# A one-core trunk layer: own buffers for value rows, stores of G behind the weights, x1 loaded early

## The chip, the core and the metric

The kernel runs on one core of one Trainium2 chip. The metric is the device time of one execution in microseconds. Three runs of the kernel before took 1787.8, 1790.84 and 1793.23 us, median 1790.84.

## The reference, cut to what matters

One layer on 512 tokens of width 2048. Four kinds of token mixing are computed first and projected back; then comes a gated feed-forward network with a convolution over three tokens. The change touches the second half:

```python
x = x + rms_norm(mixed, norm_gains[l, 1])          # this x is "x1"
h = rms_norm(x, norm_gains[l, 2])
x = x + rms_norm(conv_geglu_ffn(h, ffn_w_up[l], ffn_conv_w[l], ffn_w_down[l]), norm_gains[l, 3])

def conv_geglu_ffn(h, w_up, conv_w, w_down):
    u = causal_dwconv(h @ w_up, conv_w)            # 2 x 4096 columns
    g, up = jnp.split(u, 2, axis=-1)
    return (jax.nn.gelu(g, approximate=True) * up) @ w_down
```

The product `gelu(g) * up` is called G here: 32 rows of 128 features, each a tile of 128 partitions by 512 tokens (256 KB). Everything is in float32.

## The kernel before, in words

Features lie on partitions and tokens along the free dimension. Each weight and each operand is split into two parts, hi and lo (a cast on ScalarE, L99, L177 or L1008, and a subtraction on VectorE, L100, L178 or L1009), and each product is made of hi times hi, hi times lo and lo times hi. A plain stage (`group`, L125 to L170) loads a weight chunk of 512 KB (L98), splits it and lets TensorE run 24 or more matmuls per chunk into four PSUM tiles.

The order on TensorE is the order in which the program is written. Other engines' instructions are put in order by a scheduler with a model of times; those under `tc.high_priority` (weight loads, splits, evictions) go ahead of the rest where they are ready. `tc.issue_after(i)` puts instructions behind `i` on the same engine. Each engine, SP with its DMA issues included, takes its instructions strictly in the order so fixed: what waits holds up all behind it. A tile from a pool of n buffers has to wait until the last use of the tile that had its place is over, a store's landing included. `at` and `tick` (L107 to L114) hang side work on TensorE's progress.

The stages that matter, with their time in the profile:

- Up projection, plain (to 857 us): the first four gate rows and four value rows of G. `up_plain` (L964) runs four times: each half of the tokens H0, H1 (256 each), and in each first the gate columns (half 0), then the value columns (half 1). Evictions go to `ub` tiles (L969). When a row's second token half is there, `done` calls `conv` (L943): y = first tap (ScalarE, L948), two more taps (VectorE, L950), and for the gate the gelu (ScalarE, L953). `glu` (L957) multiplies the value by its gate (VectorE, L958) and stores the row to `g_d` in DRAM on the SP queue (L959). Gate and value rows y all come from `t2()`, the pool t2f of six buffers.
- Up projection, units 4 to 31 (857 to 1424 us): `up_unit` (L1096) makes one row of G by `seven` (L1023), a Strassen scheme of seven products on half-size blocks in the order 11, 21, T2, T1, T3, 22, T4. A product is eight pairs: eight matmuls of 512 columns (L1039) and eight of 256 (L1044). Products go to three PSUM tiles x, y, w; `take` (L1099) evicts each (ScalarE copy L1103 for a first term, VectorE adds L1105 and L1106). Weights: five plain loads by SP (L1002) and three accumulating DMAs by GpSimd (L1018) per unit. TensorE yields before T4, and there `conv` of the gate is written; `conv` of the value and `glu` follow T4. From here on `t2()` is the pool t2s and `up_tile` the pool ubs, four buffers each, made where the norms' pool `norm_ph` has just been closed (L987 to L989).
- Down projection (1424 to 1768 us): first four plain groups over G's rows 0 to 3, then `seven` again for rows 4 to 19 (`down_unit`, L1195, with operands T1, T2, T3 in the places a2, a1, a3 and spare weights in a0), then four last groups over rows 20 to 31 (`last_group`, L1219), the fourth once for each token half. `load_g` (L1135) brings G's rows back through `ystage`.
- Last norm and output: the squares of each output row (L798, ScalarE) are summed by GpSimd (L802), except the last ones, which enter TensorE's sum over partitions directly (`SumSq`, L789; the third number of its call says how many). `finish` (L1230) takes rstd (L188 to L194) and then for four blocks q loads x1 from DRAM (L1236) into one of three tiles (`x1p`, two of `ystage`), scales (L1240), adds (L1241) and stores the output (L1242), two rows at a time. `finish` runs once per token half.

Of the kernel before, what the change touches and what calls it, by code (L numbers as in the profile page):

```python
# [9 lines left out]
F32 = mybir.dt.float32  # L10
F32R = mybir.dt.float32r
AF = mybir.ActivationFunctionType
ALU = mybir.AluOpType
# [3 lines left out]
P = 128  # L17
S = 512
D = 2048
KT = D // P  # L20
# [4 lines left out]
HALVES = (slice(0, S // 2), slice(S // 2, S))  # L25
# [23 lines left out]
def trunk(ctx: ExitStack, tc: tile.TileContext, xT, params, consts, wgate, w_in, w_out, w_up0, w_up, w_dn, w_dns, out):  # L49
    nc = tc.nc  # L50
    V, A, G, T = nc.vector, nc.scalar, nc.gpsimd, nc.tensor
# [3 lines left out]
    act = ctx.enter_context(tc.tile_pool(name="act", bufs=1))  # L55
# [21 lines left out]
    def pc(name, i=0):  # L77
        return par[:, PC[name] + i:PC[name] + i + 1]
# [7 lines left out]
    w_split, w_load = [], []  # L86
# [17 lines left out]
    beside = {}  # L104
# [67 lines left out]
    def repeated(t, n):  # L172
        return t.unsqueeze(1).broadcast_to([P, n, t.shape[-1]])
# [27 lines left out]
    def traced():  # L201
        return len(nc.cur_bb.bb.instructions)

    def after_act(mark):
        held_back[:] = [i for i in list(nc.cur_bb.bb.instructions)[mark:] if type(i).__name__ == "InstActivation"]
# [13 lines left out]
    x1_d = [dram.tile([P, 2, 4, S // 2], F32, name=f"x1_d{q}") for q in range(4)]  # L219
    g_d = [dram.tile([P, S], F32, name=f"g_d{k}") for k in range(FF // P)]  # L220
# [4 lines left out]
    with ExitStack() as ph:  # L225
        big = ph.enter_context(tc.tile_pool(name="big", bufs=19))
        t2p = ph.enter_context(tc.tile_pool(name="t2p", bufs=8))
# [4 lines left out]
        def t2(dt=F32):  # L232
            return t2p.tile([P, S], dt, name="t2")
# [137 lines left out]
        for i in range(2):  # L371
            V.tensor_tensor(out=lmp[:, i * 64:(i + 1) * 64], in0=par[:, dl + 128 * i:dl + 128 * i + 64],
                            in1=par[:, dl + 128 * i + 64:dl + 128 * i + 128], op=ALU.mult)
# [9 lines left out]
        def lru(pair, xs, gs):  # L383
# [41 lines left out]
            def scan():  # L425
# [9 lines left out]
                after_act(mark)  # L435

            at(t0 + 1, conv)
            at(t0 + 9, lambda: gates(blocks[0]))
            at(t0 + 13, lambda: gates(blocks[1]))
# [181 lines left out]
        ys, vs = {}, []  # L621
# [150 lines left out]
    with ExitStack() as ph:  # L772
        wide = ph.enter_context(tc.tile_pool(name="wide", bufs=2))
        ystage = ph.enter_context(tc.tile_pool(name="ystage", bufs=2))
        up_ph = ph.enter_context(ExitStack())
        neg_p = up_ph.enter_context(tc.tile_pool(name="neg_p", bufs=1))
        t2p = up_ph.enter_context(tc.tile_pool(name="t2f", bufs=6))
        ubp = up_ph.enter_context(tc.tile_pool(name="ubp", bufs=8))

        norm_ph = up_ph.enter_context(ExitStack())  # L780
# [99 lines left out]
        H0, H1 = HALVES  # L880
# [25 lines left out]
        def split_t2():  # L906

            with tc.high_priority(offset=AHEAD):
                for i in range(2):
                    split(mg[2 + i][1], actq[i][:, 0, :, H1], actq[i][:, 1, :, H1])  # L910
# [22 lines left out]
        def up_tile():  # L933
            t = ubp.tile([P, 514], F32, name="ub")
            V.memset(t[:, 0:2], 0.0)  # L935
            return t
# [6 lines left out]
        def conv(t, half, unit, minus=False):  # L943
            def tap(i):
                n = 3 * unit + i
                return neg_w[:, n:n + 1] if minus else pc("ffn_w", 96 * half + n)
            y = t2()
            A.activation(out=y, in_=t[:, 0:512], func=AF.Copy, scale=tap(0))  # L948
            for i in (1, 2):
                V.scalar_tensor_tensor(out=y, in0=t[:, i:i + 512], scalar=tap(i), in1=y, op0=ALU.mult, op1=ALU.add)  # L950
            if half == 0:
                mark = traced()
                A.activation(out=y, in_=y, func=AF.Gelu_apprx_tanh)  # L953
                after_act(mark)
            return y

        def glu(unit, gate, value):  # L957
            V.tensor_tensor(out=value, in0=value, in1=gate, op=ALU.mult)  # L958
            nc.sync.dma_start(out=g_d[unit], in_=value)  # L959


        ub, gates = {}, {}
# [1 line left out]
        def up_plain(half, ts):  # L964
            def evac(u, ps):
                if ts.start == 0:
                    ub[half, u] = up_tile()
                t = ub[half, u]
                A.copy(out=t[:, 2 + ts.start:2 + ts.stop], in_=ps)  # L969
                return (lambda: done(u)) if ts.stop == S else None  # L970

            def done(u):
                y = conv(ub[half, u], half, u)
                if half == 0:
                    gates[u] = y
                else:
                    glu(u, gates[u], y)
            group([w_up0[half, c] for c in range(8)], act_h, act_l, natural, evac,
                  mm_tile if half == 0 else pa_tile, ts)

        for ts in HALVES:
            for half in range(2):
                up_plain(half, ts)


        split_t2()
        norm_ph.close()  # L987
        t2p = up_ph.enter_context(tc.tile_pool(name="t2s", bufs=4))
        ubp = up_ph.enter_context(tc.tile_pool(name="ubs", bufs=4))  # L989
        spare_t = wide.tile([P, 4, 4, S // 2], F32, name="mg")  # L990
        spare = [spare_t[:, i] for i in range(4)]
        turn = [0]
# [103 lines left out]
        def up_unit(unit):  # L1096
            u = [up_tile(), up_tile()]

            def take(i, ts, ps, first):  # L1099
                t = u[i][:, 2 + ts.start:2 + ts.stop]  # L1100
                with tc.high_priority(offset=AHEAD):
                    if first:
                        A.copy(out=t, in_=ps[:, 0:256])  # L1103
                    else:
                        V.tensor_tensor(out=t, in0=t, in1=ps[:, 0:256], op=ALU.add)  # L1105
                    V.tensor_tensor(out=t, in0=t, in1=ps[:, 256:512], op=ALU.add)  # L1106

            steps = seven(w_up[unit - 4], tops, take, first=unit == 4)
            next(steps)
            gate = conv(u[0], 0, unit)  # L1110
            for _ in steps:
                pass
            glu(unit, gate, conv(u[1], 1, unit, minus=True))

        for unit in range(4, FF // P):
            up_unit(unit)
        up_ph.close()


# [4 lines left out]
        m3 = [m3p.tile([P, 4, S], F32, name=f"m3{q}") for q in range(4)]  # L1124
# [10 lines left out]
        def load_g(k, t):  # L1135

            for i in range(0, 4, 2):
                with tc.high_priority(offset=AHEAD):
                    split(load_pair(k + i), t[:, 0, i:i + 2], t[:, 1, i:i + 2])
                for n in range(i, i + 2):  # L1140
                    g_h[k + n], g_l[k + n] = t[:, 0, n], t[:, 1, n]
# [66 lines left out]
            down_unit(n)  # L1208
        build_ph.close()

        x1p = ph.enter_context(tc.tile_pool(name="x1p", bufs=1))
        ph2 = ph.enter_context(tc.tile_pool(name="ph3", bufs=1))
        rstd3 = ph2.tile([P, S], F32, name="rstd3")
        load_g(20, wide.tile([P, 2, 4, S], F32R, name="xs"))
        load_g(24, wide.tile([P, 2, 4, S], F32R, name="xs"))
        load_g(28, act.tile([P, 2, 4, S], F32R, name="a1"))
        ss3 = [SumSq("q3", 4, 2), SumSq("q3", 4, 2)]

        def last_group(g, hfs, ts, pool_tile):  # L1219
            def evac(u, ps):  # L1220
                m = m3[g][:, u, ts]
                V.tensor_tensor(out=m, in0=m, in1=ps, op=ALU.add)
                done = [ss3[hf].add(m3[g][:, u, HALVES[hf]]) for hf in hfs]
                A.activation(out=m, in_=m, func=AF.Copy, scale=gain(3, 4 * g + u))
                for hf, d in zip(hfs, done):
                    if d:
                        at(clock[0] + 4, lambda hf=hf: finish(hf))
            group([w_dn[g, c] for c in range(2, 8)], g_h, g_l, range(20, 32), evac, pool_tile, ts)

        def finish(hf):  # L1230
            ts = HALVES[hf]
            ss3[hf].rstd(rstd3[:, ts])
            for q in range(4):
                x1 = (x1p if q == 0 else ystage).tile([P, 2, S], F32, name="ys")
                x1 = x1.rearrange("p a (b t) -> p (a b) t", b=2)
                nc.sync.dma_start(out=x1, in_=x1_d[q][:, hf])  # L1236
                for i in range(2):
                    ks = slice(2 * i, 2 * i + 2)
                    t, x = m3[q][:, ks, ts], x1[:, ks]
                    V.tensor_tensor(out=t, in0=t, in1=repeated(rstd3[:, ts], 2), op=ALU.mult)  # L1240
                    V.tensor_tensor(out=x, in0=t, in1=x, op=ALU.add)  # L1241
                    (nc.scalar if i else nc.sync).dma_start(out=out[hf, 2 * q + i], in_=x)  # L1242

        for g in range(3):
            last_group(g, (0, 1), ALL, mm_tile if g % 2 == 0 else pa_tile)
# [117 lines left out]
```

## Time and profile before

The profiled execution took 1794.26 us; its span, from the first to the last recorded event, is 1792.5 us.

| | |
|---|---|
| median of three runs | 1790.84 us |
| profiled execution, span | 1794.26, 1792.5 us |
| granted TensorE clock, mean | 0.986 |
| TensorE busy | 1734.0 us (97%) |
| VectorE, ScalarE, GpSimd busy | 1245.2, 896.1, 160.6 us |
| DMA | 308.13 MB, mean 172 GB/s |

The profile page gives busy times, a row of 40 slices, and the chain of waits that ended last. The trace behind it can be asked for waits by engine, for a timeline of instructions (start, duration, engine, line, operation, output<-input, and in brackets the idle time before and what ended it), and for busy times in chosen windows. PE is TensorE, PEld its weight loads, DVE VectorE, ACT ScalarE, POOL GpSimd, SPq the DMA queue of SyncE. Names are the program's: `f` is the tile of `t2()` in the feed-forward part, `ub` the tile before the convolution, `m` an output row, `ys` a staging tile, `x_d` x1 in DRAM.

### The profile page before, as it was taken

How to read it: one execution, taken by the hardware profiler on the slowest of the kernel's cores; microseconds unless marked ns; L12 is line 12 of the kernel's file. 1: busy time of each engine (PE TensorE's matmuls, PEld its weight loads, DVE VectorE, ACT ScalarE, POOL GpSimd, SP SyncE). 2: the span in 40 equal slices, each digit the busy share in tenths (PEclk: the TensorE clock that was granted, in tenths of full speed). 3: DMA queues.
4: the chain of work that ended last, by engine and by line, in shares of the span. 5: the costliest groups of instructions: out<-in, count | busy, mean ns of one | idle time of the engine just before them, and what ended most of it. 6: DMA issues, size and time to landing. Idle time of an engine off the chain costs nothing.

```text
span 1792.5 us, 25050 instructions
## 1 busy us (share of the span) xinstructions
PE 1734.0 (97%) x9504; PEld 1504.4 (84%) x9504; DVE 1245.2 (69%) x1903; ACT 896.1 (50%) x1335; POOL 160.6 (9%) x228
## 2 busy tenths in 40 slices
PE   8999999999999999999699999999999999999994
PEld 7778788887888889999588888888888878888884
DVE  7884576666666324889788888788888886775336
ACT  6442676655334334777355555555555563333432
POOL 0000011100000111100011111111111001110210
PEclk9999999999999999999899999999999999999997
DMA  7224222242222635775688888988888668876245
GB/s 259 83 94 142 82 77 77 88 144 92 95 85 92 200 105 179 235 233 178 190 212 241 229 227 228 232 228 216 232 238 224 199 196 232 217 200 196 94 129 177
DMA packets 97025, 308.13 MB, mean 172 GB/s; under 512 B 10469, under 2 KB 14821, under 8 KB 96905
## 3 DMA queue, kind: packets, MB, share of 16 engines
q1 hardware_dynamic: 80056, 247.29, 41.1%
q0 software_dynamic: 15696, 57.15, 17.3%
q10 hardware_dynamic: 1152, 2.10, 0.3%
q8 instruction: 74, 1.21, 0.3%
q14 instruction: 47, 0.38, 0.1%
HBM read 265.59 MB, written 21.24 MB: 160 GB/s over the span
## 4 chain that ended last, share of the span: by engine, by line
PE 86%; DMA 5%; DVE 3%; issue 3%; ACT 3%; SPq 0%; POOL 0%; DVEq 0%; ACTq 0%; POOLq 0%
PE mm L150 32%; PE mm L1039 25%; PE mm L1044 13%; PE pa L150 5%; PE mm L121 2%; PE mm L123 2%; PE mm L122 2%; PE pa L575 1%; DMA xs<-mg 1%; DMA a<-in_w_dns_dram 1%; DMA ys<-x_d 1%; DMA g_d<-f 1%; DVE w_lo L100 1%; DVE vd L267 1%; ACT w_hi L99 1%
## 5 line engine op out<-in xcount | busy, mean ns | idle before, releaser
L100 DVE TENSOR_TENSOR w_lo<-w_raw,w_hi 128x1024 fp32r<-128x1024 f32 (+1 forms) x207 | 253.3, 1225 | 260.9 <-PE mm L150 142.7
L150 PE MATMUL mm<-a,w_hi 128*128 128x512 f32 (+1 forms) x1744 | 373.0, 364 | 2.8 <-DVE t L318 2.1
L99 ACT CAST w_hi<-w_raw 128x1024 fp32r<-128x1024 f32 (+1 forms) x207 | 215.7, 1045 | 296.2 <-PE mm L150 216.0
L150 PEld LDWEIGHTS mm<-a,w_hi 128*128 128x128 f32 x1744 | 297.7, 189 | 53.8 <-DVE t L318 2.6
L1039 PE MATMUL mm<-a,w_hi 128*128 128x512 f32 x1088 | 276.2, 396 | 20.7 <-DVE ub L935 13.5
L1008 ACT CAST w_hi<-w_raw 128x1024 fp32r<-128x1024 f32 x145 | 152.2, 1050 | 205.7 <-PE mm L1039 168.1
L1039 PEld LDWEIGHTS mm<-a,w_hi 128*128 128x128 f32 x1088 | 197.7, 191 | 57.0 <-DVE ub L935 13.7
L1009 DVE TENSOR_TENSOR w_lo<-w_raw,w_hi 128x1024 fp32r<-128x1024 f32 x145 | 177.0, 1221 | 39.2 <-ACT w_hi L1008 38.8
L150 PE MATMUL mm<-a,w_lo 128*128 128x512 f32 (+1 forms) x872 | 198.9, 367 | 0.0
L150 PEld LDWEIGHTS mm<-a,w_lo 128*128 128x128 f32 x872 | 147.7, 190 | 24.3 <-issue 1.5
L1044 PEld LDWEIGHTS mm<-a,w_lo 128*128 128x128 f32 x1088 | 150.1, 192 | 10.8
L1044 PE MATMUL mm<-a,w_lo 128*128 128x256 f32 x1088 | 153.3, 284 | 0.0
L1039 PE MATMUL mm<-xs,w_hi 128*128 128x512 f32 x576 | 144.3, 392 | 0.2 <-DVE ub L1106 0.2
L1008 ACT CAST w_hi<-mg 128x1024 fp32r<-128x1024 f32 x84 | 87.7, 1044 | 86.8 <-PE mm L1039 84.2
L1039 PEld LDWEIGHTS mm<-xs,w_hi 128*128 128x128 f32 x576 | 103.7, 189 | 19.0 <-DVE ub L1106 0.4
L1009 DVE TENSOR_TENSOR w_lo<-mg,w_hi 128x1024 fp32r<-128x1024 f32 x84 | 102.5, 1220 | 24.3 <-ACT w_hi L1008 24.3
L1039 PE MATMUL mm<-mg,w_hi 128*128 128x512 f32 x352 | 88.9, 395 | 1.2 <-DVE m L1201 1.2
L1044 PEld LDWEIGHTS mm<-xs,w_lo 128*128 128x128 f32 x576 | 78.6, 190 | 5.6
L1106 DVE TENSOR_TENSOR ub<-ub,mm 128x256 f32<-128x256 f32 x196 | 81.2, 414 | 1.5 <-ACT ub L1103 1.5
L1044 PE MATMUL mm<-xs,w_lo 128*128 128x256 f32 x576 | 80.3, 282 | 0.0
L1039 PEld LDWEIGHTS mm<-mg,w_hi 128*128 128x128 f32 x352 | 64.0, 191 | 12.8 <-ACT a L177 1.4
L150 PE MATMUL pa<-a,w_hi 128*128 128x256 f32 (+1 forms) x512 | 72.3, 294 | 0.7 <-ACT w_hi L99 0.7
(267 smaller groups left out, 2554.8 us busy)
## 6 DMA issues: line engine op xcount, KB each, us to landing
w_raw<-in_w_up_dram SPq DMA_DIRECT2D x115, 512.0 KB, 5.1
w_raw<-in_w_in_dram SPq DMA_DIRECT2D x87, 512.0 KB, 3.5
mg<-in_w_up_dram SPq DMA_DIRECT2D x56, 512.0 KB, 4.2
w_raw<-in_w_out_dram SPq DMA_DIRECT2D x48, 512.0 KB, 3.5
w_raw<-in_w_dn_dram SPq DMA_DIRECT2D x38, 512.0 KB, 3.5
w_raw<-mg POOLq DMA_DIRECT2D x28, 512.0 KB, 5.6
mg<-in_w_up_dram POOLq DMA_DIRECT2D x27, 512.0 KB, 7.9
w_raw<-in_w_up_dram POOLq DMA_DIRECT2D x27, 512.0 KB, 9.0
```

Of the source, the lines that this page charges most:

```text
L99: w_split.append(A.copy(out=hi[:, sl], in_=raw[:, sl]))
L100: V.tensor_tensor(out=lo[:, sl], in0=raw[:, sl], in1=hi[:, sl].bitcast(F32), op=ALU.subtract)
L121: T.matmul(ps, lhsT=sh, rhs=mh, start=first, stop=False)
L122: T.matmul(ps, lhsT=sh, rhs=ml, start=False, stop=False)
L123: T.matmul(ps, lhsT=sl, rhs=mh, start=False, stop=last)
L150: T.matmul(pss[u], lhsT=a, rhs=b, start=c == 0 and kk == 0 and not low and i == 0, stop=False)
L267: V.tensor_tensor(out=ssum, in0=ssum, in1=sq, op=ALU.add)
L1008: w_split.append(A.copy(out=by4(hi), in_=v))
L1009: V.tensor_tensor(out=by4(lo), in0=v, in1=by4(hi).bitcast(F32), op=ALU.subtract)
L1039: T.matmul(ps.rearrange("p (a t) -> p a t", a=2), lhsT=hi[:, k * P:(k + 1) * P], rhs=tops[name][k], start=first and k == 0, stop=False, **kw)
L1044: T.matmul(ps[:, 0:256], lhsT=lo[:, k * P:(k + 1) * P], rhs=tops[name][k][:, 0], start=False, stop=k == 7, **kw)
L1106: V.tensor_tensor(out=t, in0=t, in1=ps[:, 256:512], op=ALU.add)
```

## The change

Four things:

1. Value rows in `conv` come from a pool of their own, `t2s` with four buffers named v2; gates stay in `t2()`, the six buffers of t2f, to the end of the up projection. For that the norms' pool is closed, and t2s and ubs are made, between the two token halves of the plain stage instead of after it.
2. `glu` no longer stores a row at once; it puts the store on a list. `store_g` issues what is on the list, behind the last weight load written so far. It is called in `up_unit` after the gate's `conv` of the next unit, and once after the last unit.
3. x1 is loaded whole, by eight DMAs of 512 KB, into two tiles in the places a0 and a2 as soon as the Strassen units of the down projection leave them, and behind the last weight load written by then. `finish` reads and writes x1 there; `x1p` is gone.
4. The last sums of squares: the last three rows of each token half, instead of the last two, go directly to TensorE's sum and not through GpSimd's running sum (five buffers instead of four).

```diff
-            y = t2()
+            y = t2() if half == 0 else t2s.tile([P, S], F32, name="v2")
...
         def glu(unit, gate, value):
             V.tensor_tensor(out=value, in0=value, in1=gate, op=ALU.mult)
-            nc.sync.dma_start(out=g_d[unit], in_=value)
+            stores.append(lambda: nc.sync.dma_start(out=g_d[unit], in_=value))
+
+        stores = []
+
+        def store_g():
+
+            with tc.issue_after(w_load[-1].ins):
+                while stores:
+                    stores.pop(0)()
...
-        for ts in HALVES:
-            for half in range(2):
-                up_plain(half, ts)
+        for half in range(2):
+            up_plain(half, H0)
+        assert not beside
+        norm_ph.close()
+        t2s = up_ph.enter_context(tc.tile_pool(name="t2s", bufs=4))
+        ubs = up_ph.enter_context(tc.tile_pool(name="ubs", bufs=4))
+        for half in range(2):
+            up_plain(half, H1)
 
         split_t2()
-        norm_ph.close()
-        t2p = up_ph.enter_context(tc.tile_pool(name="t2s", bufs=4))
-        ubp = up_ph.enter_context(tc.tile_pool(name="ubs", bufs=4))
+        ubp = ubs
...
             gate = conv(u[0], 0, unit)
+            store_g()
             for _ in steps:
                 pass
             glu(unit, gate, conv(u[1], 1, unit, minus=True))
 
         for unit in range(4, FF // P):
             up_unit(unit)
+        store_g()
         up_ph.close()
...
-        x1p = ph.enter_context(tc.tile_pool(name="x1p", bufs=1))
...
-        ss3 = [SumSq("q3", 4, 2), SumSq("q3", 4, 2)]
+        ss3 = [SumSq("q3", 5, 3), SumSq("q3", 5, 3)]
+        x1 = [act.tile([P, 4, 4, S // 2], F32, name=n) for n in ("a0", "a2")]
+        with tc.issue_after(w_load[-1].ins):
+            for hf in range(2):
+                for q in range(4):
+                    nc.sync.dma_start(out=x1[hf][:, q], in_=x1_d[q][:, hf])
...
             ss3[hf].rstd(rstd3[:, ts])
-            for q in range(4):
-                x1 = (x1p if q == 0 else ystage).tile([P, 2, S], F32, name="ys")
-                x1 = x1.rearrange("p a (b t) -> p (a b) t", b=2)
-                nc.sync.dma_start(out=x1, in_=x1_d[q][:, hf])
-                for i in range(2):
-                    ks = slice(2 * i, 2 * i + 2)
-                    t, x = m3[q][:, ks, ts], x1[:, ks]
-                    V.tensor_tensor(out=t, in0=t, in1=repeated(rstd3[:, ts], 2), op=ALU.mult)
-                    V.tensor_tensor(out=x, in0=t, in1=x, op=ALU.add)
-                    (nc.scalar if i else nc.sync).dma_start(out=out[hf, 2 * q + i], in_=x)
+            for n in range(KT // 2):
+                ks = slice(2 * (n % 2), 2 * (n % 2) + 2)
+                t, x = m3[n // 2][:, ks, ts], x1[hf][:, n // 2, ks]
+                V.tensor_tensor(out=t, in0=t, in1=repeated(rstd3[:, ts], 2), op=ALU.mult)
+                V.tensor_tensor(out=x, in0=t, in1=x, op=ALU.add)
+                (nc.scalar if n % 2 else nc.sync).dma_start(out=out[hf, n], in_=x)
```

## The prediction

> **What bounds the kernel now.** I read the page first: busy times, then the forty slices.
>
> ```profile
> span 1792.5 us, 25050 instructions
> PE 1734.0 (97%) x9504; PEld 1504.4 (84%) x9504; DVE 1245.2 (69%) x1903; ACT 896.1 (50%) x1335; POOL 160.6 (9%) x228
> ...
> PE   8999999999999999999699999999999999999994
> ```
>
> TensorE is busy almost throughout, so a change can only win where it is not: the digit 6 (the twentieth slice, 851 to 896 us) and the 4 at the end. Which waits make the holes is in the waits of TensorE from 700 us on:
>
> ```profile
> PE mm L1039 <- DVE ub L935: 13.5, 1, 13.5
> PE mm L1039 <- DVE m L1201: 6.7, 3, 3.4
> ```
>
> One wait of 13.5 us is nearly everything; the other row belongs to the down projection, which the change leaves alone. The chain of waits shows how the 13.5 us came about:
>
> ```profile
> 871.23 0.69 DVE f L958
> 871.94 11.07 DMA g_d<-f
> 883.04 0.73 ACT f L948
> ...
> 886.53 0.33 DVE ub L1106
> 886.92 3.78 PE mm L1039 x8
> 890.70 1.71 PE mm L1044 x8
> 892.41 2.17 PE mm L1039 x8
> ...
> 897.38 0.95 PE mm L1044 x8
> ...
> 915.09 1.84 PE mm L1039 x8
> ```
>
> And the timeline around it (columns: start, duration, engine, line; in brackets the idle time before and what ended it):
>
> ```profile
> 872.29 1.11 PE L1044 MATMUL mm<-xs,w_lo 128*128 128x256 f32 x8
> ...
> 877.83 0.74 DVE L950 SCALAR_TENSOR_TENSOR f<-ub,par,f 128x512 f32<-128x512 f32 x1
> 883.04 0.72 ACT L948 ACTIVATE f<-ub,par 128x512 f32<-128x512 f32 x1 [9.43 <-DMA g_d<-f]
> 883.66 0.35 ACT L1103 COPY ub<-mm 128x256 f32<-128x256 f32 x1
> 883.79 0.75 DVE L950 SCALAR_TENSOR_TENSOR f<-ub,par,f 128x512 f32<-128x512 f32 x1 [5.22 <-ACT f L948]
> ```
>
> The first convolution step (L948) of the last plain value row sits 9.43 us on ScalarE, until the store of the first row of G has landed: the six buffers of t2f hold four gates and two value rows, so this row needs a stored row's place. Behind it in ScalarE's order waits L1103, the eviction of product T1; product 22 needs that PSUM bank, so TensorE stands from 873.4 to 886.9.
>
> The other hole is the tail:
>
> ```profile
> 1767.27 1.69 POOL L802 TENSOR_TENSOR ss<-ss,q 128x256 f32<-128x256 f32 x2 [16.99 <-ACT q L798]
> 1768.20 0.71 ACT L798 ACTIVATE q<-m 128x256 f32<-128x256 f32 x2
> 1769.54 1.03 PE L812 MATMUL pa<-q,con 128*128 128x256 f32 x4
> 1772.97 0.69 DVE L1241 TENSOR_TENSOR ys<-m,ys 128x512 f32<-128x512 f32 x1 [4.72 <-DMA ys<-x_d]
> 1773.58 0.42 DVE L188 TENSOR_SCALAR f<-pa 128x256 f32<-128x256 f32 x1
> 1776.36 1.29 DVE L1240 TENSOR_TENSOR m<-m,rstd 128x512 f32<-128x512 f32 x2
> ...
> 1783.59 1.28 DVE L1240 TENSOR_TENSOR m<-m,rstd 128x512 f32<-128x512 f32 x2
> ...
> 1787.85 1.29 DVE L1241 TENSOR_TENSOR ys<-m,ys 128x512 f32<-128x512 f32 x2 [2.98 <-DMA ys<-x_d]
> ```
>
> VectorE waits twice for x1 (4.72 and 2.98 us), because its three staging tiles come free only when an output has been stored.
>
> **Part 1: own buffers for the value rows.** The plain values get four places (v2) of their own, on space that the norms' tiles leave free long before. The 9.43 us wait goes, and with it the 13.5 us. There is more: after the stop TensorE's first steps are slow. The hi and lo halves took 3.78 and 1.71, then 2.17, where 1.84 and 0.95 are the steady figures: 1.94 + 0.76 + 0.33 = 3.0 us. So the stop costs 16.5 us in all.
>
> In a sentence by itself: the Trainium skill ("TensorE: Matmul & The Clock Gate", Part 1) says that an idle window of about 3.4 us halves the clock for about another 3.4 us of work, which by that figure would be 1.7 us instead of 3.0, and the predicted time 1.3 us higher; the rows measure this very stop, so I keep 3.0.
>
> What is late next is VectorE, as the windows show (columns: PE, PEld, DVE, ACT, POOL busy with counts; granted clock; DMA share; GB/s):
>
> ```profile
> 857.40:873.40 16.00, 14.35 (x81) 12.27 (x80) 14.54 (x18) 10.72 (x16) 3.30 (x4) 1.00 0.83 218
> 873.40:886.90 13.50, 0.01 (x1) 0.00 (x0) 8.25 (x17) 1.19 (x3) 0.19 (x1) 0.59 0.74 204
> 886.90:906.60 19.70, 19.68 (x97) 17.14 (x98) 12.46 (x21) 8.58 (x12) 1.10 (x2) 0.84 0.45 130
> ```
>
> The granted clock after the stop, 0.84 over 19.7 us, is 3.2 us lost and agrees with the 3.0 above. VectorE did 14.54 + 8.25 + 12.46 = 35.25 us of work in these 49.2 us. Without stop and slow start, TensorE gets through the same products in 49.2 - 16.5 = 32.7 us, so 2.5 us of VectorE's work don't fit. If they are deferred (the convolution steps are of low priority), the cost is 0; if they are not, 2.5. I take 2.5: the two plain rows still outstanding are spread between urgent work. Gain of this part: 16.5 - 2.5 = 14.0 us.
>
> The change adds a wait: the value row of unit 4 is the fifth for four places, and its L948 waits for the store of row 0. Behind it on ScalarE are the evictions and weight casts of unit 5, and TensorE waits for those. Cover: row 0 landed at 871.94 + 11.07 = 883.0. Unit 4 had products 22 and T4 to go when TensorE stood at 873.4; two products of 2.79 us (1.84 + 0.95) put its end at 879.0 and the use of the first eviction of unit 5 two products later, at 884.6. So the wait is hidden by 1.6 us if the store lands as before, and costs its excess otherwise; zero here, the rest is the first rival. On SP nothing is moved ahead: in this first unit the stores follow loads issued long before.
>
> **Part 2: stores behind the next weights.** From unit 5 on a store is issued after the unit's last weight load instead of between its loads, and its row is held for one unit longer. A place is wanted again four units (4 x 7 products of 2.79 = 78 us) later. TensorE has no wait in that stage apart from the one above, so I cost this at 0, covered by the products' 19.5 us per unit. Last unit: the store still follows the product with the gate directly and the loads of G for the down stage wait for it as before. Gates now stay in t2f to the end, where m3 lies later; zero as well.
>
> **Part 3: x1 early, sums.** The tail without x1's waits, step by step. One add less on GpSimd frees the running sum at 1767.27 + 0.85 = 1768.1. The last square is ready at 1768.20 + 0.71 = 1768.9. One more term costs 0.52 (1.03 for two), but the first three run from 1768.1 on, so the sum ends near 1770.2 instead of 1770.6. VectorE has by then finished the first half: two adds of 0.60 (twelve steps from 1776.36 to 1783.59) were open at 1768.2. From L188 to the first scaling it is 1776.36 - 1773.58 = 2.8 us: 1770.3 + 2.8 = 1773.1. Sixteen steps at 0.60 make 9.6: 1782.7. VectorE's last step ended at 1787.85 + 0.69 = 1788.54 and the span 4.0 later, so the end is 1786.7: 5.8 us gained. A bound for the worse is how long an output takes to land:
>
> ```profile
> DMA to landing us min/median/max: 2.0/2.2/5.1
> ```
>
> If the last one takes 5.1 instead of 2.2, 2.9 of the 5.8 are lost (then 2.9). I keep 5.8, since outputs are then written without x1 being read beside them.
>
> What x1's eight loads of 512 KB collide with:
>
> ```profile
> 1611.00:1634.00 23.00, 21.82 (x126) 19.12 (x125) 19.82 (x28) 12.40 (x13) 0.86 (x1) 1.00 0.82 255
> ...
> 1620.37 0.33 SPq L98 DMA_DIRECT2D w_raw<-in_w_dn_dram  x1
> ...
> 1624.03 2.00 PE L1039 MATMUL mm<-a,w_hi 128*128 128x512 f32 x8
> ...
> 1633.84 3.82 PE L150 MATMUL mm<-xs,w_hi 128*128 128x512 f32 x16
> ...
> 1637.39 116.27 SPq L98 DMA_DIRECT2D w_raw<-in_w_dn_dram  x25
> 1643.13 1.05 ACT L99 CAST w_hi<-w_raw 128x1024 fp32r<-128x1024 f32 x1 [4.38 <-PE mm L150]
> ```
>
> At 255 GB/s one load takes 2.06 us. a0 comes free in unit 7, a2 with the end of T1 at 1624.0; then G's last rows and the first weights are on the same queue. From 1637 on weights are so far ahead that the cast waits 4.38 us for TensorE, so a late load costs nothing there. Ahead of 1634 a load can hold up a cast of G on ScalarE. Bounds 0 and four loads, 8.2; I take 1.0, half a load, being near the row with lead.
>
> **Sum.** 14.0 + 0 + 5.8 - 1.0 = 18.8 us. The profiled execution took 1794.26, 3.4 above the median of the three runs (1790.84) and just above the highest (1793.23); it would come to 1775.5. Taken from the median: 1772.0.
>
> **Rivals.** First: the stop shrinks only. If VectorE keeps its order, T1's eviction stands after the L950 at 883.79; only the 5.22 us it waited for ScalarE go. Or the wait moves: were row 0 to land at 892.9 instead of 883.0, unit 4's value row would hold TensorE 8.3 us past 884.6. Either leaves a stop of 8.3 us and the slow start: 5.2 instead of 14.0, in all 5.2 + 5.8 - 1.0 = 10.0, time 1780.8. For it speaks that VectorE works 14.54 of 16 us just ahead; against it, that evictions have priority and are put first once ScalarE isn't blocked.
>
> Second: x1 stays late. If its loads go behind the 25 weight loads of the row at 1637.39, they come only at 1753 and part of the tail remains: half of the 5.8 is lost, 1774.9.
>
> Third: x1 goes ahead of the last groups' weights, whose loads land after 3.5 us:
>
> ```profile
> w_raw<-in_w_dn_dram SPq DMA_DIRECT2D x38, 512.0 KB, 3.5
> ```
>
> Eight loads take 16.5 us from 1624.0; then a weight load (3.5) and its cast (1.05) put the first product at 1645.0 instead of 1633.84: 11.2 plus 3.0 of slow start, so 14.0 + 5.8 - 14.2 = 5.6 gained, 1785.2, at the edge of what can be told. The Trainium skill ("DMA: Bandwidth & Descriptors", Queues, rings and completion order) says that each DMA engine takes a queue's descriptors in ring order, so that what is issued first on SP is also served first; no row here contradicts it. Against this rival: weight loads carry priority, x1's don't, and the first weight load was issued at 1620.37, before a2 is free.
>
> Fourth, slower than before: weight loads, no longer held up by stores, crowd the accumulating DMAs of the up stage.
>
> ```profile
> w_raw<-mg POOLq DMA_DIRECT2D x28, 512.0 KB, 5.6
> ...
> 914.43 0.88 POOL L1018 DMA_DIRECT2D w_raw<-mg  x1 [5.77 <-DVE ub L1106]
> ```
>
> Each unit adds S2 onto A12 (issued 914.43 for the unit that begins at 915.09), and product 22 needs it five products later, at 929.0. It lands after 5.6 us; from 13.5 us on (14.6 less a cast of 1.05) TensorE waits. At 14.8 us each of 27 units would lose 1.3 us: 35 us, so 1772 + 35 = 1807. Against it: that is over twice the median, and the bytes of a unit stay the same.
>
> **How the numbers follow.** Forecast 0.64, first rival 0.18, x1 late 0.07, x1 ahead 0.07, accumulates 0.04. A difference of 0.3% (5.4 us) is about what a measurement of this kernel can tell from no change: the three runs lie 5.4 apart. The forecast, the first and the second rival are faster (0.89); of the third, at the edge, 0.03 counts as faster and 0.04 as the same; the fourth is slower. In all 0.92, 0.04 and 0.04. Range: below, all of 16.5 + 6.3 (sum of squares earlier by another 0.5) and 2.7 of spread, 1765.3; above, the first rival with 2.7 of spread, 1783.5; the third and fourth stay outside.
>
> **What would show it.** Right: no wait of TensorE above 3 us between 857 and 900; no L948 of a plain row waiting on a store; the granted clock 1.00 there; x1's loads issued between 1600 and 1640; no idle of VectorE on x1 after 1770 and about 18 us from the last square to the end (1768.9 to 1786.7). Wrong: a wait of over 5 us on L948 of unit 4's value row, a hole at 1634, or waits of TensorE in each unit of the up stage.

## The result and the profile after

The changed kernel took 1780.33 us (median of four runs, 1779.76 to 1781.07) beside 1789.69 us for the kernel before: ratio 0.9946, 95% interval 0.9928 to 0.9963. That is 9.4 us, half of the 18.8 forecast. A second measurement beside other runs of the kernel before gave 1776.65 against 1788.37 us, ratio 0.9932 (0.9919 to 0.9946). The profiled execution took 1779.76 us, its span 1778.0.

In the code of the changed kernel the lines after L957 have moved: products L1050 and L1055 (before L1039, L1044), evictions L1114, L1116, L1117 (before L1103, L1105, L1106), scaling and adding x1 L1254 and L1255.

First the page of the changed kernel, then the waits of TensorE from 700 us on:

```profile
span 1778.0 us, 24989 instructions
...
PE   8999999999999999999899999999999999999996
```

```profile
PE mm L1050 <- DVE ub L1117: 7.4, 3, 6.9
PE mm L1050 <- DVE m L1214: 3.3, 2, 2.4
```

The digit 6 in the middle became an 8, the 4 at the end a 6. The stop ahead of product 22 is not gone: 13.5 us became 6.9, and it now bears the name of an eviction. The timeline there:

```profile
873.07 1.11 PE L1055 MATMUL mm<-xs,w_lo 128*128 128x256 f32 x8
...
873.26 1.05 ACT L1019 CAST w_hi<-mg 128x1024 fp32r<-128x1024 f32 x1 [1.74 <-PE mm L1050]
873.74 1.41 DVE L950 SCALAR_TENSOR_TENSOR v<-ub,par,v 128x512 f32<-128x512 f32 x2
874.22 0.36 ACT L1114 COPY ub<-mm 128x256 f32<-128x256 f32 x1
...
875.66 1.22 DVE L1020 TENSOR_TENSOR w_lo<-mg,w_hi 128x1024 fp32r<-128x1024 f32 x1
876.80 0.75 DVE L950 SCALAR_TENSOR_TENSOR v<-ub,par,v 128x512 f32<-128x512 f32 x1
877.46 1.22 DVE L1025 TENSOR_TENSOR mg<-mg 128x1024 f32<-128x1024 f32 x1
878.60 0.69 DVE L958 TENSOR_TENSOR v<-v,f 128x512 f32<-128x512 f32 x1
879.20 0.75 DVE L950 SCALAR_TENSOR_TENSOR v<-ub,par,v 128x512 f32<-128x512 f32 x1
...
880.65 0.42 DVE L1117 TENSOR_TENSOR ub<-ub,mm 128x256 f32<-128x256 f32 x1
...
881.12 3.78 PE L1050 MATMUL mm<-a,w_hi 128*128 128x512 f32 x8 [6.94 <-DVE ub L1117]
```

No L948 waits for a store any more, and ScalarE has copied T1's first half by 874.6. But VectorE adds the second half only at 880.65, after the taps (L950) and multiplications (L958) of the plain rows 1 and 2, the taps of row 3 and two steps on weights (L1020, L1025; rows are counted from 0). VectorE is busy throughout, 6.88 of the 6.90 us from 874.2 to 881.1, mostly with taps and multiplications of plain rows that nobody needs yet. The slow start, 3.78 for eight matmuls, is the same as before; the granted clock over the 19.6 us behind the stop was 0.85 (0.84 before). The wait that the change added didn't show: unit 4's value row found its place stored:

```profile
891.48 0.72 ACT L948 ACTIVATE v<-ub,neg_w 128x512 f32<-128x512 f32 x1 [0.74 <-DVE ub L1117]
```

The tail of the changed kernel:

```profile
1760.61 0.40 ACT L798 ACTIVATE q<-m 128x256 f32<-128x256 f32 x1
...
1761.80 0.42 DVE L188 TENSOR_SCALAR f<-pa 128x256 f32<-128x256 f32 x1 [0.79 <-PE pa L812]
...
1764.60 1.29 DVE L1254 TENSOR_TENSOR m<-m,rstd 128x512 f32<-128x512 f32 x2
...
1773.03 1.29 DVE L1255 TENSOR_TENSOR a<-m,a 128x512 f32<-128x512 f32 x2
```

After L1254 has begun VectorE never waits: sixteen steps, one every 0.60 us. The outputs land in 2.0 to 2.2 us, none in 5.1. And x1's loads (tile `a<-x_d`) went between the weights, one to three at a time:

```profile
1609.29 0.32 SPq L1234 DMA_DIRECT2D a<-x_d  x1
...
1637.85 0.43 SPq L1234 DMA_DIRECT2D a<-x_d  x1
1642.91 101.96 SPq L98 DMA_DIRECT2D w_raw<-in_w_dn_dram  x22
```

Single runs of one kernel differ by up to 10 us (1783.31 to 1793.46 for the kernel before, in one series of nine), much of it ahead of the place of the change: the first product of unit 4 began between 853.5 and 858.6 us in the fourteen traces that follow. So I compare stretches that end and begin with the same instruction. "Units 4+5" is from the first product of unit 4 to that of unit 6 (39.1 us without any wait), "up" from the first product of unit 4 to the first of the plain down groups, "down" the Strassen units of the down projection, "end" from the first product of the last groups to the end of the span, all in us:

| kernel | units 4+5 | up | down | end |
|---|---|---|---|---|
| before | 57.6 | 566.4 | 166.5 | 158.7 |
| before, second trace | 55.6 | 564.5 | 165.4 | 158.5 |
| changed | 51.5 | 560.3 | 163.5 | 153.0 |
| changed, second trace | 50.4 | 559.2 | 164.5 | 153.0 |
| value rows and stores alone | 50.1 | 558.9 | 164.8 | 158.5 |
| x1 and sums alone | 56.1 | 564.9 | 167.0 | 152.8 |
| changed, two direct sums | 51.2 | 560.0 | 163.6 | 153.5 |
| changed, stores at once | 50.8 | 559.6 | 165.7 | 153.0 |
| the same, second trace | 51.4 | 560.2 | 163.1 | 153.0 |
| two rows deferred | 46.1 | 554.9 | 163.7 | 153.4 |
| three rows deferred, order | 45.0 | 556.0 | 165.5 | 153.0 |
| plain multiplications on GpSimd | 49.1 | 557.9 | 164.6 | 153.0 |
| six taps left out | 45.9 | 554.7 | 163.9 | 153.1 |
| rows spread, order | 45.7 | 554.5 | 166.3 | 153.8 |

### The profile page after: what moved, and what is told of

It reads as the page before. It is cut to its first block, busy times and chain, and to the rows that moved or that the text cites. A ratio compares the mean times of both kernels' runs of the same rounds, so it can differ in the third digit from the quotient of the medians.

```text
span 1778.0 us, 24989 instructions
## 1 busy us (share of the span) xinstructions
PE 1735.0 (98%) x9508; PEld 1504.6 (85%) x9508; DVE 1245.7 (70%) x1903; ACT 896.4 (50%) x1335; POOL 159.1 (9%) x226
## 4 chain that ended last, share of the span: by engine, by line
PE 87%; DVE 4%; issue 4%; ACT 2%; DMA 2%; POOL 0%; POOLq 0%; SPq 0%; DVEq 0%; ACTq 0%
PE mm L150 33%; PE mm L1050 25%; PE mm L1055 13%; PE pa L150 5%; PE mm L121 2%; PE mm L123 2%; PE mm L122 2%; PE pa L575 1%; DMA xs<-mg 1%; DVE w_lo L100 1%; ACT w_hi L99 1%; DVE w_lo L1020 1%; PE pa L680 1%; DVE vd L267 0%; DMA a<-in_w_dns_dram 0%
## 5 line engine op out<-in xcount | busy, mean ns | idle before, releaser
L1050 PE MATMUL mm<-a,w_hi 128*128 128x512 f32 x1088 | 275.4, 395 | 12.1 <-DVE ub L1117 7.2
L1050 PEld LDWEIGHTS mm<-a,w_hi 128*128 128x128 f32 x1088 | 197.2, 190 | 48.5 <-DVE ub L1117 7.6
L1020 DVE TENSOR_TENSOR w_lo<-w_raw,w_hi 128x1024 fp32r<-128x1024 f32 x145 | 177.2, 1222 | 37.3 <-ACT w_hi L1019 37.1
L1055 PEld LDWEIGHTS mm<-a,w_lo 128*128 128x128 f32 x1088 | 150.0, 192 | 11.1 <-DVE w_lo L1020 0.3
L1055 PE MATMUL mm<-a,w_lo 128*128 128x256 f32 x1088 | 153.4, 284 | 0.0
L1050 PE MATMUL mm<-xs,w_hi 128*128 128x512 f32 x576 | 144.3, 392 | 0.2 <-DVE ub L1117 0.2
L1020 DVE TENSOR_TENSOR w_lo<-mg,w_hi 128x1024 fp32r<-128x1024 f32 x84 | 102.6, 1221 | 25.2 <-ACT w_hi L1019 25.2
L1050 PEld LDWEIGHTS mm<-xs,w_hi 128*128 128x128 f32 x576 | 103.6, 189 | 19.0 <-DVE ub L1117 0.4
L1050 PE MATMUL mm<-mg,w_hi 128*128 128x512 f32 x352 | 88.6, 394 | 1.3 <-ACT xs L177 1.1
L1055 PEld LDWEIGHTS mm<-xs,w_lo 128*128 128x128 f32 x576 | 78.6, 190 | 5.6
L1117 DVE TENSOR_TENSOR ub<-ub,mm 128x256 f32<-128x256 f32 x196 | 81.5, 416 | 1.5 <-ACT ub L1114 1.5
L1055 PE MATMUL mm<-xs,w_lo 128*128 128x256 f32 x576 | 80.3, 282 | 0.0
L1050 PEld LDWEIGHTS mm<-mg,w_hi 128*128 128x128 f32 x352 | 63.6, 190 | 13.0 <-ACT xs L177 1.3
```

The lines of the kernel that those rows point to most:

```text
L1020: V.tensor_tensor(out=by4(lo), in0=v, in1=by4(hi).bitcast(F32), op=ALU.subtract)
L1050: T.matmul(ps.rearrange("p (a t) -> p a t", a=2), lhsT=hi[:, k * P:(k + 1) * P], rhs=tops[name][k], start=first and k == 0, stop=False, **kw)
L1055: T.matmul(ps[:, 0:256], lhsT=lo[:, k * P:(k + 1) * P], rhs=tops[name][k][:, 0], start=False, stop=k == 7, **kw)
```

## The experiments

**Each part alone.** Two kernels, each with one half of the diff: the first has the changed `conv`, `glu`, `store_g` and pools with the tail of before, the second the new tail with the old up projection.

```diff
+ x1 = [act.tile([P, 4, 4, S // 2], F32, name=n) for n in ("a0", "a2")]     # second kernel only
+ y = t2() if half == 0 else t2s.tile([P, S], F32, name="v2")               # first kernel only
```

> The changed kernel with the tail of the kernel before: own buffers for value rows and stores behind the weights, but x1 through the staging tiles and two direct sums. Theory (the stop of TensorE in the first Strassen unit shrinks from 13.5 to about 7 us because VectorE's fixed order puts T1's eviction behind the plain rows' taps; the slow start of 3 us stays): this part alone gains 5 to 6.5 us, 1783 to 1785, and the tail from the last square to the end is about 23.5 us again. Rival (the gain of the whole change is the tail's alone, and the shorter stop is made up elsewhere in the up stage): within 2 us of the kernel before, 1788 to 1791.

> The kernel before with x1 loaded early into a0 and a2 and three direct sums; value rows and stores as before. Theory: the tail's waits on x1 go, last square to end about 17 us instead of 23.6, gain 5 to 6.5 us, 1783 to 1785, and the stop of 13.5 us is there as before. Rival (x1's loads cost the last groups what the tail gains): below 2 us gained, 1788 to 1790, with waits of TensorE between 1600 and 1650 us.

Measured: 1784.31 (ratio 0.9974, 0.9962 to 0.9985) and 1784.89 (0.9977, 0.9965 to 0.9989) beside 1789.27: 5.0 and 4.4 us, 9.3 together, where the whole gained 9.4 in its first measurement and 11.7 in its second. The 4.4 are below the 5 to 6.5 expected of the second part. The table is the surer witness that the parts don't touch each other: "up" falls by some 6 us with the first alone and by 5 to 6 with both, "end" by 5.8 with the second alone and 5.6 with both. The rivals fall.

**Two plain rows deferred.** The taps and the multiplication of rows 2 and 3 are put behind the eviction of product 22 of unit 4:

```diff
+ if half == 1 and u >= 2:
+     late.append(lambda: glu(u, gates[u], conv(ub[half, u], half, u)))
+     return
...
  next(steps)
+ with tc.issue_after(evicted[-1].ins):
+     while late:
+         late.pop(0)()
```

> The changed kernel, with the taps and the multiplication of the last two plain value rows put behind the eviction of product 22 of unit 4 on VectorE; nothing is left out. Theory (VectorE's order): T1's eviction comes right after its copy on ScalarE, the stop of about 7 us shrinks to below 2, the slow start goes too: 6 to 9 us less than the changed kernel, 1771 to 1774. Rival (TensorE waits for operands or weights of product 22 at that time, the eviction is only the last of several): the stop stays above 4 us, 1778 to 1781.

Measured: 1776.37 us, 4.0 less than the changed kernel's first median, but only 0.3 less than its second, and above the 1771 to 1774 expected; "up" is the surer witness, 554.9 instead of 559.7 (mean of six). The stop shrank from 6.94 to 2.58, not below 2, and the start after it stayed slow, if less. TensorE in this kernel (products L1053) and what precedes it on the others:

```profile
874.38 1.05 ACT L1022 CAST w_hi<-mg 128x1024 fp32r<-128x1024 f32 x1 [1.74 <-PE mm L1053]
...
875.34 0.36 ACT L1117 COPY ub<-mm 128x256 f32<-128x256 f32 x1
...
876.27 1.22 DVE L1023 TENSOR_TENSOR w_lo<-mg,w_hi 128x1024 fp32r<-128x1024 f32 x1
...
877.40 0.41 DVE L1120 TENSOR_TENSOR ub<-ub,mm 128x256 f32<-128x256 f32 x1
...
877.87 2.54 PE L1053 MATMUL mm<-a,w_hi 128*128 128x512 f32 x8 [2.58 <-DVE ub L1120]
```

What is left has to do with the order too: a weight cast for unit 5 stands ahead of T1's copy on ScalarE, as it did in the changed kernel (873.26 there), waiting for TensorE itself, and its subtraction ahead of T1's eviction on VectorE. Priority is no protection: both are of high priority, and the order is fixed ahead.

**The taps left out.** As a test of the same cause without moving anything, rows 1 to 3 keep only their first tap:

```diff
- for i in (1, 2):
+ for i in (1, 2) if half == 0 or unit == 0 or unit > 3 else ():
```

> The changed kernel without the second and third tap of the plain value rows 1 to 3 (that part of the convolution is left out). Theory (low-priority work of VectorE stands ahead of T1's eviction): six steps of 0.66 us go, the wait of TensorE before product 22 shrinks from 6.9 to 1.5 to 3.5 us. Rival (the eviction waits for something else, the steps only fill the time): the wait stays above 5 us.

The kernel took 1773.32 us in its one execution. The wait fell to 2.44 us, as the theory had it:

```profile
875.39 3.40 PE L1050 MATMUL mm<-a,w_hi 128*128 128x512 f32 x8 [2.44 <-DVE ub L1117]
```

Units 4 and 5 took 45.9 us instead of 51.5. Six steps of about 0.7 us, which have nothing to do with product T1, were worth 4.5 us of TensorE's waiting.

**Three rows deferred, and the order mended on both engines.**

```diff
- if half == 1 and u >= 2:
+ if half == 1 and u >= 1:
...
- o11 = operand(a11)                       # unit 5 alone
+ with tc.issue_after(copied[2].ins), tc.issue_after(evicted[3].ins):
+     o11 = operand(a11)
```

> The changed kernel with the taps and multiplications of three plain value rows (1 to 3) behind the eviction of product 22, and with the first split of unit 5's weights put behind T1's eviction, on ScalarE as on VectorE. Theory (the order on both engines, fixed ahead, is the whole of the stop): T1's copy follows its product at once, the wait of TensorE before product 22 falls below 1 us and no slow start follows; unit 4 then takes about 22.5 us from its first product to that of unit 5, 4 us less than with two rows deferred, and the kernel 1771 to 1774. Rival (something else, a weight or an operand, is late by then too): a wait of 2 us or more stays in unit 4 or at the start of unit 5, 1775 to 1778.

Half a hit. Product 22 followed T3 without a gap, and unit 4 took 22.3 us, as expected. But TensorE stood later, in unit 5 and unit 6:

```profile
871.57 2.00 PE L1053 MATMUL mm<-a,w_hi 128*128 128x512 f32 x8
...
877.58 1.05 ACT L1022 CAST w_hi<-w_raw 128x1024 fp32r<-128x1024 f32 x1 [5.71 <-DMA w_raw<-in_w_up_dram]
...
878.66 1.22 DVE L1023 TENSOR_TENSOR w_lo<-w_raw,w_hi 128x1024 fp32r<-128x1024 f32 x1 [3.53 <-ACT w_hi L1022]
...
885.80 2.11 PE L1053 MATMUL mm<-a,w_hi 128*128 128x512 f32 x8 [2.89 <-DVE ub L1124]
...
915.82 2.11 PE L1053 MATMUL mm<-a,w_hi 128*128 128x512 f32 x8 [1.82 <-DVE ub L1124]
```

Up took 556.0 us, 1.1 more than with two rows; the median, 1775.92, is 0.7 below that of the changed kernel on the same chip (1776.65), which these runs can't tell from nothing, and within the rival's 1775 to 1778. So the order is the cause of the stop, but not all of what is lost. VectorE has about 41.4 us of work in units 4 and 5 (41.41 us busy in the changed kernel, 41.30 with two rows deferred), and TensorE without waits needs 39.1, so some of it is late somewhere. And here VectorE itself stood 3.53 us: the next subtraction in its order waited for a cast, and the cast for a weight load that landed 22.6 us after unit 4 had begun (21.1 to 23.3 us in all traces). With the stop gone the kernel reaches this load before it has landed, and the second half of product 22's eviction and all the deferred work stood behind it.

**Less work for VectorE.** In the kernel with two rows deferred, GpSimd multiplies the four plain rows:

```diff
- V.tensor_tensor(out=value, in0=value, in1=gate, op=ALU.mult)
+ (G if unit < 4 else V).tensor_tensor(out=value, in0=value, in1=gate, op=ALU.mult)
```

> The kernel with two plain value rows deferred, and with the multiplication of the four plain rows on GpSimd instead of VectorE; nothing is left out. Theory (VectorE has more to do in units 4 and 5 than fits, which deferring only moves): 2.4 us less on VectorE shorten the stretch from the first product of unit 4 to the end of the up projection by 1.5 to 4 us, from 554.9 to 551 to 553.5 us; about 1772 to 1775. Rival (GpSimd's accumulating DMAs are held up behind its multiplications): 555 us or more, waits of TensorE on weights in units 4 and 5.

1777.52 us, up 557.9: the theory is refuted, and the rival has the number right, but its reason doesn't show. TensorE's only wait on weights in units 4 and 5 is the one of 1.68 us at unit 4's second product, which every kernel has (1.5 to 2.2 us). The timeline of this kernel:

```profile
873.30 1.22 DVE L1023 TENSOR_TENSOR w_lo<-w_raw,w_hi 128x1024 fp32r<-128x1024 f32 x1
873.48 2.19 POOL L958 TENSOR_TENSOR v<-v,f 128x512 f32<-128x512 f32 x1 [0.86 <-DVE v L950]
...
882.15 1.23 DVE L1023 TENSOR_TENSOR w_lo<-w_raw,w_hi 128x1024 fp32r<-128x1024 f32 x1 [3.60 <-ACT w_hi L1022]
...
886.58 1.70 POOL L958 TENSOR_TENSOR v<-v,f 128x512 f32<-128x512 f32 x1 [1.92 <-DVE v L950]
...
887.08 1.76 DVE L950 SCALAR_TENSOR_TENSOR f<-ub,par,f 128x512 f32<-128x512 f32 x1
...
891.04 1.27 POOL L958 TENSOR_TENSOR v<-v,f 128x512 f32<-128x512 f32 x1 [2.76 <-DVE v L950]
891.22 2.18 DVE L1023 TENSOR_TENSOR w_lo<-w_raw,w_hi 128x1024 fp32r<-128x1024 f32 x1
```

Beside GpSimd's 1.70 us a tap takes 1.76 us instead of 0.75, and a subtraction 2.18 instead of 1.22; where VectorE's step had begun first (873.30), it kept its 1.22 and GpSimd's took 2.19 instead of 1.3. So part of what is taken from VectorE is given back by making it slow. It isn't all: the order changed elsewhere too. Product 22 now followed without a stop, unit 4 took 22.6 us, and as with three rows deferred VectorE then stood (3.60 us) on a weight load, with the deferred taps behind that. TensorE stood 3.98 us at the start of unit 5's product T2, with a slow start after it, and unit 5 took 26.5 us instead of 19.55. The slow tap ahead of that stop accounts for 1.0 us of it; how the rest divides isn't shown.

**Rows spread.** Row 2 behind product 22 of unit 4, row 3 behind that of unit 5, the order mended as above:

```diff
- while late:
-     late.pop(0)()
+ late.pop(0)()
```

> The changed kernel with the third plain value row's taps behind product 22 of unit 4 and the fourth's behind product 22 of unit 5, and the first split of unit 5's weights behind T1's eviction on both engines; nothing is left out. Theory (VectorE's work beyond what a unit has room for, some 3 us a unit, must be spread): the sum of units 4 and 5 from first product to first product is below 45 us (39.1 without any wait; 45.0 with three rows at once, 46.1 with two, 51 in the changed kernel), the time 1772 to 1776. Rival (what is gained in unit 4 always comes back in unit 5): 45 us or more, 1775 to 1778.

1772.77 us, ratio to before 0.9904 (0.9886 to 0.9922), the lowest median of all. Units 4 and 5 took 45.7 us, above the 45 that the theory asked for. The three waits left there are of three kinds, a weight cast, VectorE's order and an eviction:

```profile
861.37 2.82 PE L1053 MATMUL mm<-a,w_hi 128*128 128x512 f32 x8 [2.19 <-ACT w_hi L1022]
875.18 2.11 PE L1053 MATMUL mm<-a,w_hi 128*128 128x512 f32 x8 [0.81 <-DVE ub L935]
887.69 2.11 PE L1053 MATMUL mm<-a,w_hi 128*128 128x512 f32 x8 [1.07 <-DVE ub L1124]
```

The first of them was 1.57 in the changed kernel and stands ahead of the place of the edit; the two others sum to 1.9 where three rows at once left 2.9 in the same stretch. Whether this kernel is really faster than that with two rows deferred these medians don't settle.

**The place of the stores.** Stores of G at once instead of behind the next weights, twice, the second time beside the changed kernel itself:

```diff
- stores.append(lambda: nc.sync.dma_start(out=g_d[unit], in_=value))
+ nc.sync.dma_start(out=g_d[unit], in_=value)
```

> The changed kernel with each row of G stored at once, as before, and not behind the next weights. Theory (the place of the stores is worth nothing, since TensorE doesn't wait in the units): within 1.5 us of the changed kernel, 1779 to 1782, and the stop of about 7 us is the same. Rival (stores between the loads hold up weights at the beginning of the units): the stop is longer by 2 us or more, 1782 to 1786.

> The changed kernel once more, beside the others on this chip: 1779 to 1782 by every theory, so that the place of the stores can be judged on one chip.

> Stores of G at once, once more, beside the changed kernel on the same chip. Theory (the place is worth nothing): the medians differ by less than 1 us. Rival (storing at once is really better, as 1778.05 against 1780.33 on two chips would have it): 1.5 to 3 us less than the changed kernel.

The first time 1778.05 us, 2.3 below the changed kernel's first median and outside the 1.5 expected; side by side 1776.81 against 1776.65. The place is worth nothing that these runs can tell, and the stop has the same length (6.92 us). The changed kernel's 1776.65 missed the 1779 to 1782 that every theory gave it: medians of four and five runs of one kernel on two occasions differ by 3.7 us here.

**Two direct sums.**

```diff
- ss3 = [SumSq("q3", 5, 3), SumSq("q3", 5, 3)]
+ ss3 = [SumSq("q3", 4, 2), SumSq("q3", 4, 2)]
```

> The changed kernel with two direct sums and four buffers as before, x1 still early. Theory (one add of GpSimd less ahead of the last sum is worth about half a microsecond): from the last square to the end 0.3 to 0.8 us more than in the changed kernel, its time the same within 1.5 us, 1779 to 1782. Rival (the direct sums are an essential part of the gain at the end): 2 us or more slower, 1782 to 1784.

1780.61 us, 4.0 above the changed kernel beside it, more than the theory's 1.5 and within the rival's bound; but the trace bears out the theory. TensorE's sum waits for GpSimd again:

```profile
1758.91 0.70 PE L812 MATMUL pa<-ss,con 128*128 128x256 f32 x2 [1.70 <-POOL ss L802]
```

From the last square to the end it took 18.5 us instead of 17.0, but the last square came 0.9 earlier after the start of the last groups, so "end" differs by 0.5 us. The two profiled executions (1778.46 and 1776.20 us) differ ahead of the tail for the rest: unit 4 began at 856.1 instead of 854.3 and "up" took 0.9 more, "down" 0.9 less, which the sums can't touch. I take the 4.0 of the medians for scatter of that kind; it isn't shown for the runs without a trace.

**The kernel before, once more.**

> The kernel before once more, for a second trace of it. By every theory: unit 4 from its first product to that of unit 5 36.5 to 38.1 us, from the last groups' first product to the end 158 to 159 us. If the down projection's Strassen units take 166 to 167 us again (163 to 166 in all runs with own value buffers), the change gains some 2 us there too; if they take 163 to 165, that difference is scatter.

Span 1788.0. Unit 4 took 36.1 us, just below the 36.5 to 38.1 expected. The stop was 10.73 us here, 13.14 in the kernel with the new tail alone, 13.51 in the trace that the prediction used. Its length follows that of the first row's store:

```profile
870.95 9.77 DMA g_d<-f
```

```profile
880.75 0.72 ACT L948 ACTIVATE f<-ub,par 128x512 f32<-128x512 f32 x1 [6.66 <-DMA g_d<-f]
```

The store took 9.77 us to land instead of 11.07 (10.72 where the stop was 13.14), and TensorE came to the place 1.8 us later in the unit, after a slow start at product 21: both shorten the stop. "Down" took 165.4 us, between the other traces of the old up projection (166.5, 167.0) and the eleven with own value rows (163.1 to 166.3, mean 164.5): whether the change gains there stays open.

## Why the prediction was half right

**What bounds the kernel**: right. The two holes were where the waits named them, and the rest of the trace stayed as it was.

**Part 1, the wait on the store**: the wait went as forecast, L948 of the last plain row doesn't wait any more. The term was mis-sized: 14.0 us forecast, 5.0 measured for the part alone, 5.6 in "up" (mean of six traces with unchanged order, 559.7, against 565.3 of three with the old). The step that failed is the sentence against the first rival, "that evictions have priority and are put first once ScalarE isn't blocked". VectorE's instructions kept their order but for one multiplication, which went behind the eviction: the order is fixed ahead. That the low-priority steps stand there because by the scheduler's model the eviction isn't ready yet is my reading, which no run shows; in the trace it was ready 6 us earlier. So the stop became 6.9 us, not 0, and with it the slow start of some 3 us stayed, which I had counted as gained. The rival's own figures, a stop of 8.3 us and 5.2 us gained, were nearly it; its chance of 0.18 was too small. The row that should have said so was in the trace of before: between 877.83 and 886.53 VectorE had only L950s, L958s and memsets to do ahead of L1106.

The 2.5 us of VectorE's excess were rightly worked out: about 41.4 us of work against 39.1 in units 4 and 5. But they are not all that is lost there: with the rows deferred or spread, 45.0 to 46.1 us instead of 39.1 remain for the two units, about 1.7 of it the wait for a weight cast that was there before, and with three rows deferred VectorE's own wait on a weight load, 3.53 us, is in it, which the forecast didn't have. The forecast also took the stop of one trace, 13.5 us, as the kernel's; two more traces with the old up projection show 13.1 and 10.7.

**Part 2, the stores**: 0 forecast, 0 measured. The added wait was covered, as worked out, and not only because a stop remained: with three rows deferred and no stop in unit 4, the store of row 0 landed at 882.09 and unit 4's value row began at 882.39, held up by an eviction and not by the store. The fourth rival fell too: the up stage behind units 4 and 5 took 508.8 us before and after.

**Part 3**: 5.8 us forecast for the tail; from the last groups' first product to the end it is 158.7 to 153.0, or 5.7, and the sums' share of it 0.5. The steps hold one by one: L188 to the first scaling 2.8 us, sixteen steps in 9.7 us, outputs landing as forecast. That the sum came out so near is in part luck. The row at 1787.85 in the trace of before holds two additions, so VectorE's last step ended at 1789.14 and not at 1788.54, and the same sum read rightly gives 6.4 us. From the end of the last square to the end of the span 23.6 became 17.0, 6.6 us less; but with three direct sums the last square came 0.9 us later after the start of the last groups (with two, at the old place), which the forecast didn't have. The 1.0 us for x1's loads beside the weights was not needed: they were issued between 1609 and 1638 with the weights between them, and ahead of the last groups TensorE waited once, 1.14 us, where the two traces of before have waits of 1.18 and 1.02. The rivals that put x1 too late or ahead of the weights fell.

**The numbers**: 1772.0 forecast, 1780.33 measured, inside 1765.3 to 1783.5. The range held since the first rival was in it. Of the signs of being right, two failed: TensorE waited 6.9 us, and the granted clock behind the wait was 0.85 and not 1.00.

## What to carry to other kernels

When a wait is removed, look at what stands between the waiting instruction and its next use on every engine in the fixed order: work placed there because the wait left room for it stays there when the wait is gone. Low priority does not make an instruction step aside once the order is written. Then look for what was covered by the wait: here a weight load, which nobody had to wait for as long as TensorE stood. And judge a change of half a per cent by stretches between the same two instructions in several traces, not by the difference of two single executions: here the two profiled ones differed by 14.5 us, the medians by 9.4.

## What the runs showed of the hardware

The slow start does not need a stop of 13 us, and a stop of about 2 us doesn't settle whether it comes. In the down projection's first unit the same eight matmuls, 2.00 us at a granted clock of 1.00, took 2.09 after a wait of 2.08 us in the kernel before (granted clock over these 2.09 us 1.00), and 3.42 after a wait of 2.08 us in the kernel with the new tail alone (0.55 over these 3.42 us):

```profile
1475.11 2.09 PE L1039 MATMUL mm<-a,w_hi 128*128 128x512 f32 x8 [2.08 <-DVE m L1201]
```

```profile
1472.02 3.42 PE L1039 MATMUL mm<-a,w_hi 128*128 128x512 f32 x8 [2.08 <-DVE m L1201]
```

The Trainium skill ("TensorE: Matmul & The Clock Gate", Part 1) speaks of idle windows of about 3.4 us that run freely. That would explain that one and the same wait is caught by a window or not, but not that 2.08 us suffice; the measurement decides.

GpSimd's multiplication of two rows slowed steps of VectorE that began after it, a tap from 0.75 to 1.76 us and a subtraction from 1.22 to 2.18 us; where VectorE's subtraction began first, GpSimd's step took 2.19 us instead of 1.3 and the subtraction kept its 1.22.
